# A four-layer diffusion backbone: attention probabilities scaled on GpSimd by a scalar per partition, and the sink logit taken as the first value of the fused row minimum

## The chip, the cores and the metric

The kernel runs on one core of one Trainium2 chip. The profile names the core's engines PE (TensorE matmuls), PEld (TensorE weight loads), DVE (VectorE), ACT (ScalarE), POOL (GpSimd) and SP (the queue that issues the DMAs). The metric is the device time of one launch in microseconds. Three runs of the kernel before took 2281.0, 2281.58 and 2281.96 us; the median is 2281.58 us.

## The reference, cut to what matters

Two token streams, 256 latent tokens and 256 context tokens of width 1024, go through four layers. Layer i mixes tokens by its kind (differential attention, neighbourhood attention, windowed grouped-query attention with a sink, differential attention again) and then runs a SwiGLU FFN; each half is normalised before and after. The change touches the softmax of the second and the third layer.

```
# layer 1, neighbourhood attention (16 heads of 64)
s_nb = q . k(neighbours) + relative-position bias;  s_cx = q . k(context)
p = softmax(concat[s_nb, s_cx]);  out = p . v
# layer 2, windowed attention (16 heads, 4 key heads) with a sink logit per head
s_band = where(valid, s_band, -inf)
snk = broadcast_to(sink_f, (B, KV, G, QB, 1))
p = softmax(concat([s_band, s_cx, snk], axis=-1))
out = p[..., :nband] @ v_band + p[..., nband:nband + C] @ v_cx      # the sink's column has no value row
# context rows attend to context keys alone, with the same sink in layer 2
```

## The kernel before, in words

The text calls the layers 0 to 3 (kinds A, B, C, A), the context stream c and the latent stream l. Tile names end in the same letters: `bkc` and `bkl` are PSUM banks, `x_c` and `x_l` the residual streams, `h` the normalised input in two halves. Each matrix product is made of three matmuls (`mm3`, lines 508 to 510): high part times high part, high times low, low times high. So every weight tile of 128x1024 is loaded by SP, split by ACT into a rounded part `wh` and by DVE into the rest `wl` (line 522).

A layer runs over units, one weight tile each: value, query and key projections, then the output projection (`o`), then 22 gate, 22 up and 22 down units of the FFN. In layers 1 and 2 each query and key pair of units is followed by `att_bc` for two heads. A head of the latent stream has two query tiles of 128 rows with 512 keys each; a head of the context stream has one tile in which two query blocks of 128 rows stand side by side with 256 keys each. One tile goes this way: scores on PE (887, 888); for the latent stream one fused DVE operation that adds the bias or mask, writes the sum and its negated row minimum (995), for the context stream a row maximum (895); in layer 2 a small DVE operation that takes the sink into that column (1001); exponential and row sum on ACT; in layer 2 the sink's exponential and an add (1018); reciprocal (1020); the scaling of the probabilities; four PE transposes (907); a split into two parts by ACT and DVE (915); the product with the values (1037, 1038) and the sum of its halves (1043). Before the change the scaling stood on POOL for the context stream (1023); for the latent stream the table `SPLIT` put it on DVE (1026) for both query tiles of layer 1 and for tile 0 of layer 2, and on ACT for tile 1 of layer 2.

After the output projection and after the FFN each stream passes a norm: ACT squares the output and DVE multiplies it by the gate (798), POOL makes the reciprocal root (690, 692), DVE adds to the residual (804), ACT squares again, POOL makes the second root, DVE scales (725), PE transposes (738), and ACT and DVE split the result into `h` (752). PE can only go on with that stream's next products after that; until then it works on the other stream.

The order of all instructions on every engine is made by a list scheduler in the program (`Plan`): the code records operations with an engine, a planned duration, a priority and the buffers that they touch; `run` schedules them four times with priorities mixed from the earlier passes, and the pass with the least planned end is emitted. Each engine executes its own list strictly in order. So a change of one planned duration moves instructions in all layers, on all engines.

Of the kernel before, what the change touches and what calls it, by code (L numbers as in the profile page):

```python
# [14 lines left out]
ALU = mybir.AluOpType  # L15
AX = mybir.AxisListType

P = 128
# [39 lines left out]
ALONE = 2  # L58
QK_BOTH = False
LATE = 5  # L60
SPLIT = {"B": [0, 1], "C": [0]}
BOOST = {"A": -4.0, "B": 8.0, "C": 16.0, "N": 20.0, "F": -8.0, "X": 28.0}
ADA_BANK = "bkc"
# [262 lines left out]
def t_dve(n, fast=False, extra=0.0):  # L326
    return 0.07 + (0.00052 if fast else 0.00104) * n + extra
# [3 lines left out]
def trunk(ctx: ExitStack, tc: tile.TileContext, a: dict, out: bass.AP, layers=tuple(range(DEPTH)), info=None):  # L331
    nc = tc.nc
# [43 lines left out]
    def fixed(shape, dt=F32, name="k"):  # L376
        return Buf("fixed", ap=const.tile(list(shape), dt, name=name, tag=name))
# [12 lines left out]
    def op(eng, dur, fn, reads=(), writes=(), p=None, also=()):  # L390
        r = [x if isinstance(x, tuple) else (x, None) for x in reads]
        w = [x if isinstance(x, tuple) else (x, None) for x in writes]
        return plan.op(eng, dur, fn, prio() if p is None else p, r, w, also)
# [18 lines left out]
    def dve(fn, dur, reads, writes, p=None):  # L412
        return op("dve", dur, fn, reads, writes, p)
# [4 lines left out]
    def load_fixed(shape, src, name):  # L418
        b = fixed(shape, name=name)
        dma(lambda: b.ap, lambda: src, 4 * int(np.prod(shape)), [], [b])  # L420
        return b
# [29 lines left out]
    late = {}  # L451

    def late_consts():

        late["cosT"] = load_fixed((P, T), a["cosT"], "cosT")
        late["sinT"] = load_fixed((P, T), a["sinT"], "sinT")
        late["sink"] = load_fixed((P, 16), a["c_sink"].to_broadcast([P, 16]), "sink")
        sub = late["subln"] = load_fixed((P, 2), a["sublnT"], "subln")
        lamv = Buf("f2")
        v4 = lambda: lamv.ap[:].rearrange("p (j f d) -> p j f d", j=2, f=4)  # L460
# [461 lines left out]
    def part(x, i, nk):  # L922
        return x.ap[:, i * nk:(i + 1) * nk]
# [50 lines left out]
    def att_bc(S, s, j, L):  # L974
        kind = MIXERS[L]
# [5 lines left out]
        nk = T * len(kp[0])  # L981
        nkt = nk // P
        sinks = kind == "C"
        vals = values(s)
        qs, o = S.qs, S.o
        for m in range(2):
            pt = pt_tiles(s, nkt)
            head = 2 * j + m
            for qts in blocks(s):
# [2 lines left out]
                e, l, nm, r = Buf("f2", cap=("e" + s, CAP_E[s])), Buf("col"), Buf("col"), Buf("col")  # L992
                sb = scores(s, qs, m, qts, kp[m], e)
                if plus:
                    dve(lambda e=e, sb=sb, plus=plus, nm=nm: nc.vector.tensor_tensor_reduce(
                        e.ap, sb.ap, plus.ap, -1.0, 3e38, ALU.add, ALU.min, nm.ap[:, 0:1]), t_dve(512), [sb, plus], [e, nm])
                else:
                    neg_max(sb, nm, nq)
                if sinks:
                    sink = late["sink"]  # L1000
                    dve(lambda nm=nm, head=head, nq=nq: nc.vector.scalar_tensor_tensor(
                        nm.ap[:, 0:nq], sink.ap[:, head:head + 1].to_broadcast([P, nq]), -1.0, nm.ap[:, 0:nq], ALU.mult, ALU.min),
                        0.08, [sink], [nm])
# [16 lines left out]
                dve(lambda r=r, l=l, nq=nq: nc.vector.reciprocal(r.ap[:, 0:nq], l.ap[:, 0:nq]), 0.1, [l], [r])  # L1020
                for i in range(nq):
                    if s == "c":
                        op("pool", 0.7, lambda e=e, r=r, i=i: nc.gpsimd.tensor_tensor(
                            part(e, i, nk), part(e, i, nk), r.ap[:, i:i + 1].to_broadcast([P, nk]), ALU.mult), [r], [(e, i)])
                    elif qts[0] in SPLIT[kind]:
                        dve(lambda e=e, r=r: nc.vector.tensor_scalar(e.ap, e.ap, r.ap[:, 0:1], None, ALU.mult),
                            t_dve(nk, True, 0.06), [r], [e])
                    else:
                        act(lambda e=e: e.ap, lambda e=e: e.ap, AF.Copy, t_act(nk, False, 1), [r], [e],
                            scale=lambda r=r: r.ap[:, 0:1])  # L1030
# [324 lines left out]
    for L in layers:  # L1355
        kind = MIXERS[L]
# [151 lines left out]
```

## Time and profile before

| What | Value |
|---|---|
| median of 3 runs | 2281.58 us (2281.0 to 2281.96) |
| the profiled execution | 2279.39 us |
| its span, first to last instruction | 2277.3 us |
| mean granted TensorE clock | 0.992 |
| busy: PE, PEld, DVE, ACT, POOL | 97%, 85%, 72%, 47%, 10% |
| on the chain that ended last: PE, DVE, ACT, POOL | 83%, 9%, 4%, 1% |

The profiled execution is 2.1 us longer than its span and 2.2 us below the median. The busy shares are means over stages that differ much: in the FFN stages PE is busy without a break, in the attention of layer 2 DVE is nearly so.

### The profile page before, as it was taken

What the parts mean: (1) busy time and instruction counts of PE and PEld (TensorE: products, weight loads), DVE (VectorE), ACT (ScalarE), POOL (GpSimd) and SP (SyncE); (2) the same over time, 40 slices, a digit from 0 to 9 for tenths busy, and PEclk for the clock granted to TensorE, in tenths of its full rate; (3) what the DMA queues carried; (4) which work ended last, traced back from release to release, by engine and by line L of the source; (5) the groups of instructions that cost most, each with busy time, mean ns of one, the idle gap of its engine ahead of it and who ended that gap; (6) DMA issues with size and microseconds to landing.
All of it is one profiled execution on the core that took longest, in us unless ns stands there. A gap on an engine that the chain in (4) does not pass through costs nothing.

```text
span 2277.3 us, 35872 instructions
## 1 busy us (share of the span) xinstructions
PE 2212.1 (97%) x13236; PEld 1929.4 (85%) x13236; DVE 1642.2 (72%) x3145; ACT 1062.0 (47%) x2245; POOL 221.6 (10%) x300
## 2 busy tenths in 40 slices
PE   7999999999999999999999999999999998998998
PEld 5889888888878998888878898888887887997997
DVE  4988698887354888878773489988778335896454
ACT  4478642223344776522233368862223324685443
POOL 0111110000010221200000133010000001320000
PEclk9999999999999999999999999999999999999999
DMA  8643366664233343556542430256654242434654
GB/s 294 214 131 121 98 202 221 213 215 149 86 123 93 103 114 107 179 193 210 191 153 93 138 87 19 75 160 204 213 187 172 87 136 75 128 114 148 185 184 141
DMA packets 369279, 338.92 MB, mean 149 GB/s; under 512 B 33120, under 2 KB 282960, under 8 KB 369104
## 3 DMA queue, kind: packets, MB, share of 16 engines
q1 hardware_dynamic: 369104, 336.63, 46.6%
q8 instruction: 104, 1.70, 0.3%
q14 instruction: 71, 0.58, 0.1%
HBM read 321.77 MB, written 1.17 MB: 142 GB/s over the span
## 4 chain that ended last, share of the span: by engine, by line
PE 83%; DVE 9%; ACT 4%; issue 2%; POOL 1%; DMA 0%; SPq 0%; DVEq 0%; ACTq 0%; POOLq 0%
PE bkl L508 19%; PE bkl L509 19%; PE bkl L510 19%; PE bkc L508 6%; PE bkc L509 6%; PE bkc L510 6%; ACT f L408 2%; PE bkl L907 1%; DVE r L915 1%; ACT r L408 1%; DVE wl L522 1%; PE bkc L636 1%; DVE col L895 1%; PE bkl L738 1%; DVE r L856 1%
## 5 line engine op out<-in xcount | busy, mean ns | idle before, releaser
L408 ACT ACTIVATE wh<-wr 128x1024 fp32r<-128x1024 f32 x380 | 402.6, 1061 | 843.1 <-PE bkl L509 499.1
L522 DVE TENSOR_TENSOR wl<-wr,wh 128x1024 fp32r<-128x1024 f32 x380 | 472.6, 1245 | 350.7 <-ACT wh L408 349.5
L508 PE MATMUL bkl<-h,wh 128*128 128x256 f32 (+1 forms) x1872 | 637.0, 340 | 0.0
L509 PE MATMUL bkl<-h,wh 128*128 128x256 f32 (+1 forms) x1872 | 632.2, 338 | 0.0
L510 PE MATMUL bkl<-h,wl 128*128 128x256 f32 (+1 forms) x1872 | 632.2, 338 | 0.0
L629 DVE SCALAR_TENSOR_TENSOR f<-f,cs,f 128x512 f32<-128x512 f32 x556 | 386.4, 745 | 6.0 <-DMA f<-in_ada_w 5.3
L508 PEld LDWEIGHTS bkl<-h,wh 128*128 128x128 f32 x1872 | 355.5, 190 | 41.5 <-issue 3.7
L510 PEld LDWEIGHTS bkl<-h,wl 128*128 128x128 f32 x1872 | 355.3, 190 | 37.5
L509 PEld LDWEIGHTS bkl<-h,wh 128*128 128x128 f32 x1872 | 355.5, 190 | 36.9
L508 PE MATMUL bkl<-wh,h 128*128 128x512 f32 (+1 forms) x560 | 219.1, 391 | 0.0
L509 PE MATMUL bkl<-wl,h 128*128 128x512 f32 (+1 forms) x560 | 216.7, 387 | 0.0
L510 PE MATMUL bkl<-wh,h 128*128 128x512 f32 (+1 forms) x560 | 216.6, 387 | 0.0
L508 PE MATMUL bkc<-wh,h 128*128 128x512 f32 (+1 forms) x472 | 186.6, 395 | 0.2 <-ACT j L408 0.2
L510 PE MATMUL bkc<-wh,h 128*128 128x512 f32 (+1 forms) x472 | 184.1, 390 | 1.8 <-DVE h L702 1.0
L509 PE MATMUL bkc<-wl,h 128*128 128x512 f32 (+1 forms) x472 | 183.9, 390 | 1.7 <-DVE wl L522 1.7
L690 POOL TENSOR_SCALAR col<-col 128x1 f32<-128x1 f32 x58 | 37.2, 642 | 1477.2 <-ACT j L408 1432.4
L509 PE MATMUL bkc<-h,wh 128*128 128x256 f32 x496 | 142.6, 287 | 6.6 <-DVE h L752 6.4
L508 PE MATMUL bkc<-h,wh 128*128 128x256 f32 x496 | 144.0, 290 | 0.2
L510 PE MATMUL bkc<-h,wl 128*128 128x256 f32 x496 | 141.7, 286 | 0.0
L508 PEld LDWEIGHTS bkl<-wh,h 128*128 128x128 f32 x560 | 105.4, 188 | 22.0 <-ACT h L408 0.8
L510 PEld LDWEIGHTS bkl<-wh,h 128*128 128x128 f32 x560 | 105.3, 188 | 21.4
L509 PEld LDWEIGHTS bkl<-wl,h 128*128 128x128 f32 x560 | 105.4, 188 | 19.8
(213 smaller groups left out, 3400.8 us busy)
## 6 DMA issues: line engine op xcount, KB each, us to landing
wr<-in_ffn_w SPq DMA_DIRECT2D x264, 512.0 KB, 3.7
f<-in_ada_w SPq DMA_DIRECT2D x384, 256.0 KB, 4.3
wr<-in_a_wqkv SPq DMA_DIRECT2D x48, 512.0 KB, 3.7
f<-gd SPq DMA_DIRECT2D x54, 256.0 KB, 4.8
r<-r SPq DMA_DIRECT2D x96, 128.0 KB, 2.3
wr<-in_b_wqkv SPq DMA_DIRECT2D x24, 512.0 KB, 3.6
wr<-in_a_wo SPq DMA_DIRECT2D x16, 512.0 KB, 3.5
wr<-in_c_wqkv SPq DMA_DIRECT2D x12, 512.0 KB, 3.7
```

Of the source, the lines that this page charges most:

```text
L408: nc.scalar.activation(o(), i(), func, **k)
L508: nc.tensor.matmul(o, lh, rh, start=first, stop=False)
L509: nc.tensor.matmul(o, lh, rl, start=False, stop=False)
L510: nc.tensor.matmul(o, ll, rh, start=False, stop=last)
L522: dve(lambda: nc.vector.tensor_tensor(l.ap, raw.ap, f32(h.ap[:]), ALU.subtract), t_dve(1024), [raw, h], [l], p)
L629: dve(lambda b=b, raw=raw, c=c: nc.vector.scalar_tensor_tensor(b.ap, raw.ap, c(), b.ap, ALU.mult, ALU.add), t_dve(512, extra=0.06), [raw, ...
L636: nc.tensor.matmul(acc.ap[32 * j:32 * j + 32, u * 256:(u + 1) * 256], lhs, tiles[j // 2].ap[:, (j % 2) * 256:(j % 2 + 1) * 256], start=fir ...
L690: op("pool", 0.25, lambda: nc.gpsimd.tensor_scalar(r.ap[:, 1:2], ss.ap[:, 0:1], ss.ap[:, 1:2], D * EPS, ALU.add, ALU.add), [ss], [r])
L738: nc.tensor.transpose(tp.ap[:, c0:c0 + P], xn[t, k // 4].ap[:, (k % 4) * P:(k % 4 + 1) * P], ident.ap)
L856: dve(lambda r0=r0, r1=r1, m=m: nc.vector.scalar_tensor_tensor(qs.ap[r1, m, :], src()[r0], QSCALE, f32(qs.ap[r0, m, :]), ALU.mult, ALU.sub ...
L895: dve(lambda: nc.vector.tensor_reduce(nm.ap[:, 0:n], b.ap[:].rearrange("p (i k) -> p i k", i=n), AX.X, ALU.max, negate=True), t_dve(512), ...
L907: nc.tensor.transpose(tp.ap[:, to * P:(to + 1) * P], e.ap[:, c * P:(c + 1) * P], ident.ap)
```

## The change

The diff has three edits.

1. A tile `negsink` holds the negated sink, made once by DVE. For latent rows of layer 2 the fused operation takes the head's column of it as the first value of its running minimum, in place of the constant 3e38, and the small operation of line 1001 goes for them (32 of 48; the 16 of the context stream stay).
2. The context stream's scaling on POOL (64 operations of 128x256 in layers 1 and 2 together) becomes a tensor_scalar with a column as its scalar, in place of a tensor_tensor with the column broadcast. Its planned duration goes from 0.7 to 0.5.
3. A table `ON_POOL` puts the scaling of latent query tile 0 in layer 2 (16 operations of 128x512) on POOL, planned at 0.85; these were on DVE.

```diff
+ON_POOL = {"B": [], "C": [0]}
...
+        negs = late["negsink"] = fixed((P, 16), name="negsink")
+        dve(lambda: nc.vector.tensor_scalar(negs.ap, late["sink"].ap, -1.0, None, ALU.mult), 0.1, [late["sink"]], [negs])
...
-                    dve(lambda e=e, sb=sb, plus=plus, nm=nm: nc.vector.tensor_tensor_reduce(
-                        e.ap, sb.ap, plus.ap, -1.0, 3e38, ALU.add, ALU.min, nm.ap[:, 0:1]), t_dve(512), [sb, plus], [e, nm])
+                    first = (lambda head=head: late["negsink"].ap[:, head:head + 1]) if sinks else lambda: 3e38
+                    dve(lambda e=e, sb=sb, plus=plus, nm=nm, first=first: nc.vector.tensor_tensor_reduce(
+                        e.ap, sb.ap, plus.ap, -1.0, first(), ALU.add, ALU.min, nm.ap[:, 0:1]), t_dve(512),
+                        [sb, plus] + ([late["negsink"]] if sinks else []), [e, nm])
...
-                if sinks:
-                    sink = late["sink"]
+                sink = late["sink"]
+                if sinks and not plus:
...
-                        op("pool", 0.7, lambda e=e, r=r, i=i: nc.gpsimd.tensor_tensor(
-                            part(e, i, nk), part(e, i, nk), r.ap[:, i:i + 1].to_broadcast([P, nk]), ALU.mult), [r], [(e, i)])
+                        op("pool", 0.5, lambda e=e, r=r, i=i: nc.gpsimd.tensor_scalar(
+                            part(e, i, nk), part(e, i, nk), r.ap[:, i:i + 1], None, ALU.mult), [r], [(e, i)])
+                    elif qts[0] in ON_POOL[kind]:
+                        op("pool", 0.85, lambda e=e, r=r: nc.gpsimd.tensor_scalar(e.ap, e.ap, r.ap[:, 0:1], None, ALU.mult), [r], [e])
```

The scheduler makes a new order from this. Three places are shown; the line numbers of the new kernel are a few higher (798, 804, 725 and 738 become 801, 807, 728 and 741).

On DVE at the end of the attention of layer 1, the context stream's norm before the FFN: the residual adds (804) and the scalings (725) of `x_c`. Before:

```order
L798 TENSOR_TENSOR f_10166<-bkc,f_10011 128x512
L804 SCALAR_TENSOR_TENSOR x_c<-f_10037,col,x_c 128x512
L804 SCALAR_TENSOR_TENSOR x_c<-f_10166,col,x_c 128x512
L798 TENSOR_TENSOR f_10192<-bkc,f_10011 128x512
L804 SCALAR_TENSOR_TENSOR x_c<-f_10054,col,x_c 128x512
L804 SCALAR_TENSOR_TENSOR x_c<-f_10192,col,x_c 128x512
L725 SCALAR_TENSOR_TENSOR f_10189<-x_c,col,f_10023 128x512
L725 SCALAR_TENSOR_TENSOR f_10204<-x_c,col,f_10035 128x512
L522 TENSOR_TENSOR wl<-wr,wh 128x1024 x2
```

And now, from the first residual add on (1000 is the fused minimum, 1034 the scaling of a latent tile, 918 and 1051 the split and the sum of halves of a latent head):

```order
L807 SCALAR_TENSOR_TENSOR x_c<-f_9918,col,x_c 128x512
L807 SCALAR_TENSOR_TENSOR x_c<-f_10051,col,x_c 128x512
L807 SCALAR_TENSOR_TENSOR x_c<-f_9920,col,x_c 128x512
L807 SCALAR_TENSOR_TENSOR x_c<-f_10066,col,x_c 128x512
L1026 RECIPROCAL col<-col 128x1
L1051 TENSOR_TENSOR ool<-bkl,f_10118 64x256
L1000 ISA f_10069,col<-bkl,f_122 128x512
L1000 ISA col 128x1
L1034 TENSOR_SCALAR f_10060<-f_10060,col 128x512
L728 SCALAR_TENSOR_TENSOR f_10110<-x_c,col,f_9905 128x512
L918 TENSOR_TENSOR r_10079<-bkl,r_10078 128x2x128
L728 SCALAR_TENSOR_TENSOR f_10120<-x_c,col,f_9905 128x512
```

Before, the last latent heads were done when the norm of the context stream ran, and 42 latent products of the output projection stood on PE beside it. Now the norm runs among the operations of the last latent heads.

On PE at the end of the output projection of layer 2, the transposes of the two norms (738, now 741; `bkc` and `bkl` tell the streams). Before:

```order
L738 MATMUL bkc<-ident,f_16155 128x128
L738 MATMUL bkc<-ident,f_16170 128x128
L508 MATMUL bkl<-wh,h_78 128x512
L509 MATMUL bkl<-wl,h_78 128x512
L510 MATMUL bkl<-wh,h_78 128x512
L508 MATMUL bkl<-wh,h_79 128x512
L509 MATMUL bkl<-wl,h_79 128x512
L510 MATMUL bkl<-wh,h_79 128x512
L738 MATMUL bkc<-ident,f_16167 128x128
L738 MATMUL bkc<-ident,f_16181 128x128
```

And now:

```order
L741 MATMUL bkc<-ident,f_16124 128x128
L741 MATMUL bkc<-ident,f_16200 128x128
L741 MATMUL bkl<-ident,f_16266 128x128
L741 MATMUL bkl<-ident,f_16273 128x128
L741 MATMUL bkl<-ident,f_16266 128x128
```

Before, 48 latent products stood ahead of the context stream's first transposes, and 60 products of the FFN's first context unit between its last ones and those of the latent stream. Now 30 latent products stand ahead, and the transposes of the two streams follow each other.

On POOL in the attention of layer 2, where the context stream's scalings (1023, now 1029), the rotary products (844 and 845, now 847 and 848) and the new scalings of latent tiles (1032) share one queue. Before, in the middle of the stage:

```order
L1023 TENSOR_TENSOR f_14359<-f_14359,col 128x256 x2
L844 TENSOR_TENSOR f_14487<-f_14487,sinT 128x256
L1023 TENSOR_TENSOR f_14390<-f_14390,col 128x256 x2
L845 TENSOR_TENSOR f_14476<-f_14476,f_14487 128x256
L1023 TENSOR_TENSOR f_14420<-f_14420,col 128x256 x2
L1023 TENSOR_TENSOR f_14479<-f_14479,col 128x256 x2
```

And now, at about the same place:

```order
L1032 TENSOR_SCALAR f_14274<-f_14274,col 128x512
L847 TENSOR_TENSOR f_14416<-f_14416,sinT 128x256
L1029 TENSOR_SCALAR f_14321<-f_14321,col 128x256 x2
L848 TENSOR_TENSOR f_14441<-f_14441,f_14416 128x256
L1032 TENSOR_SCALAR f_14303<-f_14303,col 128x512
L1029 TENSOR_SCALAR f_14342<-f_14342,col 128x256 x2
```

The latent scalings are new in the queue: each stands in turn with context scalings and rotary pairs, and one rotary pair still has a context tile's scaling between its two operations.

## Rows read from the trace of the kernel before

**Rows 1.** The page, its first part: the span; then busy time, share of the span and instructions of PE, PEld, DVE, ACT and POOL.

```profile
span 2277.3 us, 35872 instructions
PE 2212.1 (97%) x13236; PEld 1929.4 (85%) x13236; DVE 1642.2 (72%) x3145; ACT 1062.0 (47%) x2245; POOL 221.6 (10%) x300
```

**Rows 2.** Busy time by stage. Columns: window, its length, then PE, PEld, DVE, ACT and POOL busy (instructions), granted clock, DMA share, GB/s. The windows are the passage from layer 0 to 1; the attention of layer 1; its passage to the FFN; the attention of layer 2; its passage to the FFN; the passage from layer 2 to 3.

```profile
640.00:700.00 60.00, 56.73 (x279) 45.59 (x278) 35.76 (x62) 28.00 (x60) 10.66 (x16) 0.94 0.36 109
740.00:880.00 140.00, 138.45 (x1140) 136.09 (x1140) 124.23 (x302) 106.50 (x283) 35.53 (x53) 1.00 0.39 104
880.00:945.00 65.00, 62.59 (x353) 54.60 (x352) 49.82 (x100) 36.80 (x89) 15.06 (x20) 0.97 0.52 158
1360.00:1480.00 120.00, 111.15 (x811) 103.58 (x810) 113.67 (x382) 101.80 (x297) 23.99 (x35) 0.99 0.15 48
1480.00:1525.00 45.00, 42.67 (x272) 37.94 (x271) 38.60 (x74) 29.67 (x73) 11.01 (x16) 1.00 0.54 170
1868.00:1900.00 32.00, 25.76 (x113) 21.28 (x112) 24.76 (x39) 18.04 (x46) 10.11 (x16) 0.89 0.27 88
```

**Rows 3.** The operations that the change touches, and their neighbours on POOL. The first three rows are groups by line and shape over the whole run: busy us, mean ns | idle before. The others are single lines: count, then minimum, median and maximum in ns, first and last start in us.

```profile
L1026 DVE TENSOR_SCALAR f<-f,col 128x512 f32<-128x512 f32 x48 | 25.9, 541 | 0.8
L1001 DVE SCALAR_TENSOR_TENSOR col<-sink,col 128x1 f32<-128x1 f32 x32 | 4.3, 150 | 0.0
L995 DVE CUSTOM_DVE_ANT_0 f<-bkl,f 128x512 f32<-128x512 f32 x64 | 43.4, 681 | 4.4 <-POOL f L1068 1.7 <-PE bkl L888 1.3 <-issue 1.2
L1023 POOL TENSOR_TENSOR f<-f,col x64: 607/613/1700, 736.4 to 1409.2; 128x256 f32<-128x256 f32 x64
L690 POOL TENSOR_SCALAR col<-col x58: 299/302/2476, 10.3 to 2271.0; 128x1 f32<-128x1 f32 x58
L844 POOL TENSOR_TENSOR f<-f,sinT x42: 723/739/1802, 98.5 to 2037.9; 128x256 f32<-128x256 f32 x42
L845 POOL TENSOR_TENSOR f<-f,f x42: 723/874/1932, 99.9 to 2039.1; 128x256 f32<-128x256 f32 x42
```

**Rows 4.** Who PE waited for in the attention of layer 2 (1360 to 1480 us): total us, times, longest us.

```profile
PE bkl L907 <- DVE f L1026: 2.2, 1, 2.2
PE bkc L509 <- DVE wl L522: 1.7, 1, 1.7
PE bkl L887 <- DVE col L995: 1.7, 1, 1.7
PE bkc L907 <- POOL f L1023: 1.7, 2, 1.2
```

**Rows 5.** PE in order of time at the end of layer 2's output projection: start us, length, line and tiles, count [idle before, and who ended it]. The first row is the first of 48 latent products right behind the last context product, 1506.20 is the last latent product; L738 are the transposes of the two norms.

```profile
1491.47 0.39 PE L508 MATMUL bkl<-wh,h 128*128 128x512 f32 x1
...
1502.36 1.03 PE L738 MATMUL bkc<-ident,f 128*128 128x128 f32 x8
...
1506.20 0.39 PE L510 MATMUL bkl<-wh,h 128*128 128x512 f32 x1
...
1511.07 0.39 PE L509 MATMUL bkc<-h,wh 128*128 128x256 f32 x1 [1.74 <-DVE h L752]
...
1516.71 0.27 PE L738 MATMUL bkl<-ident,f 128*128 128x128 f32 x1
1517.44 0.98 PE L738 MATMUL bkl<-ident,f 128*128 128x128 f32 x7 [0.45 <-DVE f L725]
```

**Rows 6.** The same view at the end of layer 1's output projection. The first row is the last context product.

```profile
917.57 0.39 PE L510 MATMUL bkc<-wh,h 128*128 128x512 f32 x1
...
927.32 1.04 PE L738 MATMUL bkc<-ident,f 128*128 128x128 f32 x8
...
934.71 0.39 PE L509 MATMUL bkc<-h,wh 128*128 128x256 f32 x1 [0.86 <-DVE h L752]
...
936.81 0.58 PE L509 MATMUL bkc<-h,wh 128*128 128x256 f32 x1 [1.49 <-DVE h L752]
```

**Rows 7.** The same view at the other passages: from layer 0 to 1 (first two rows), from layer 2 to 3 (next two), and in layer 3, where only the latent stream is left, from its last output product to its transposes (last two).

```profile
673.36 0.29 PE L594 MATMUL bkc<-ident,c 128*32 128x128 f32 x1 [2.49 <-DVE c L603]
...
675.08 0.80 PE L510 MATMUL bkc<-wh,h 128*128 128x512 f32 x1 [0.78 <-DVE h L752]
...
1884.57 0.33 PE L738 MATMUL bkc<-ident,f 128*128 128x128 f32 x1 [4.04 <-DVE f L725]
1887.10 2.61 PE L738 MATMUL bkc<-ident,f 128*128 128x128 f32 x11 [2.20 <-DVE f L725]
...
2071.42 0.39 PE L510 MATMUL bkl<-wh,r 128*128 128x512 f32 x1
2078.84 0.45 PE L738 MATMUL bkl<-ident,f 128*128 128x128 f32 x1 [7.03 <-DVE f L725]
```

**Rows 8.** DVE operations of the norms and of a latent head's end, by line and shape over the whole run: busy us, mean ns | idle before.

```profile
L804 DVE SCALAR_TENSOR_TENSOR x_c<-f,col,x_c 128x512 f32<-128x512 f32 x24 | 16.8, 747 | 1.8 <-POOL col L692 1.8
L725 DVE SCALAR_TENSOR_TENSOR f<-x_c,col,f 128x512 f32<-128x512 f32 x24 | 17.0, 746 | 5.0 <-POOL col L692 5.0
L752 DVE SCALAR_TENSOR_TENSOR h<-bkc,mod,h 128x256 fp32r<-128x256 f32 x48 | 20.8, 475 | 1.6 <-ACT h L408 1.5
L915 DVE TENSOR_TENSOR r<-bkl,r 128x256 fp32r<-128x256 f32 x192 | 73.6, 415 | 6.6 <-ACT r L408 5.7
L1043 DVE TENSOR_TENSOR ool<-bkl,f 64x256 f32<-64x256 f32 x32 | 13.2, 413 | 3.4 <-ACT f L408 2.9
```

## The prediction

> **What bounds the kernel now.** I read the page's first part, then the busy time by stage, then PE in order of time where a stage shows PE idle. PE is busy 97% of the span [rows 1], and the FFN stages are solid, so a change can only win or lose where PE stands still or runs at its lower clock. Those places are few [rows 2]. The attention of layer 1 leaves PE 1.6 of 140 us idle. The attention of layer 2 leaves 8.9 of 120 us, while DVE is busy 113.7 us (95%) and ACT 101.8 (85%): this stage is DVE's. The passages between stages make up most of the rest: 3.3 us idle from layer 0 to 1, 2.4 at the end of layer 1's attention, 2.3 at that of layer 2, 6.2 from layer 2 to 3; in layer 3 one piece alone has 7.0 us [rows 7].
>
> At a passage PE waits for a norm. In layer 3 nothing covers it, and PE stands from the last output product to the first transposes, 2071.42 to 2078.84: 7.4 us for a bare norm of one stream [rows 7]. With two streams sharing DVE, ACT and POOL it is longer: from the last context product, just ahead of 1491.47, to 1502.36, at most 11 us, in layer 2, and from the last latent product at 1506.20 to 1517.44, 11.2 us [rows 5]. What stands on PE between a stream's last product and its transposes is its cover. The 48 latent products take 10.9 us (0.227 each), and there PE doesn't wait at all; 44 products of 256 columns take 5.6 us from 1511.07 to 1516.71, 0.13 each [rows 5].
>
> Idle time also costs clock: the granted clock is 0.94 over 60 us where PE stood 2.49 and 0.78 us, 0.97 over 65 us behind 0.86 and 1.49 us, 0.89 over 32 us behind 4.04 and 2.20 us, but 1.00 behind 1.74 and 0.45 us [rows 2, 5 to 7]. [...]
>
> **The change, part by part.** *Layer 2's attention.* DVE loses 16 scalings at 0.541 us, 8.7 us, and 32 sink minima at 0.150 us, 4.8 us [rows 3]: 13.5 of 113.7 us. The fused minimum reads its first value from a column in place of a constant; it took 0.681 us [rows 3], and I leave that. From below nothing less is to be expected; from above take the step between the two DVE forms of 512 columns with and without a column of which I have rows, 0.746 against 0.681 [rows 3, 8]: 0.07 us, 2 us over 32. PE waited here once 2.2 us for a DVE scaling, and 1.7 us each for a weight split and a row minimum [rows 4], all in DVE's queue. PE's idle 8.9 us and the 1.2 us that clock 0.99 costs are all that can come back. Two things limit it. ACT's 101.8 us don't shrink: in 106.5 us they would be 96%, so ACT is late next. And in the new order 84 output products, not 60, stand behind the last value product, so 5.5 us of PE work no longer fills the attention; 13.5 less 5.5 leaves 8 us. I take -5 us, from -10 to +4.
>
> The 16 scalings on POOL have no row of their own. Nearest from below is a tensor_scalar of one column, 0.302 us; from above two context tiles of 256, 2 x 0.613 us; with the fixed 0.30 us counted once, 0.93 us [rows 3]. I take 0.8 us, near the upper row since that one also moves a whole tile: 13 us more on POOL, which is busy 24 of 120 us [rows 2]. The head waits 0.3 us longer than the DVE scaling took, plus what POOL has in hand: behind the waiting scaling in its queue stand rotary pairs (0.74 and 0.87 us) and context scalings, and for these wait the next scores and context transposes. [...]
>
> *Context scalings.* 64 on POOL now take 0.613 us; the new form lies between one column's 0.302 and a rotary product's 0.739 us [rows 3]. At 0.5 us, midway from the first to today's, a tile of two saves 0.2 us. In layer 1 PE has 1.6 us idle to give; in layer 2 PE waited 1.7 us for them [rows 4], counted above. I take -0.5 us, from -1 to +0.5. `negsink` is one operation of 16 columns, once: nothing.
>
> *What the new order does to the passages.* No edit touches them, but the scheduler has moved their cover. I count products in the new order and set them against the norm's 7.4 to 11 us.
>
> From layer 0 to 1 the context stream's cover grows from 30 to 36 wide products and the latent one's from 12 to 24: 1.4 and 2.7 us against 3.3 us idle [rows 7]. Idle falls to 0 or 1 us, and part of the 3.6 us of clock comes back: -5 us, from -1 to -6.9.
>
> End of layer 1. Before, the context norm had 42 latent products beside it, 9.7 us from 917.57 to 927.32, and PE's two waits were for `h` [rows 6]. Now it has 8 score products, 16 head transposes, 24 value products and its own first 8 transposes until its second transposes: 32 x 0.13 and 24 x 0.13 [rows 5], 7.2 us. DVE, from the first residual add to the last scaling of that norm, has 4 adds, 4 scalings (725) and 2 parts of `h` of the norm itself, and of the latent heads 9 splits of 256 columns, 2 sums, 2 scalings and 1 fused minimum: 2.99 + 2.98 + 0.95 + 3.74 + 0.83 + 1.08 + 0.68 = 13.3 us [rows 3, 8]. PE would idle 6.1 us. Behind it 60 latent products cover the rest of the context norm, so the two waits for `h` (2.4 us [rows 6]) go; the latent norm then has 72 narrow products, 9.2 us, against 7.4 to 11, about 1 us short. 6.1 - 2.4 + 1 = +5 us, from 0 (DVE has started early) to +9 (clock lost as well).
>
> End of layer 2. The context norm has 30 products, 6.8 us, in place of 48. The latent norm has 16 transposes, 2 us, in place of 60 products and 4 transposes; 7.4 to 11 us less 2 leaves 5.4 to 9 us idle where there were 2.2 [rows 5]. That is 3.2 to 7 us more; I take 4, and 2 us for the clock, since the passages with over 2.3 us idle lost 2 to 3.6 us and this one none. +6 us, from +3 to +10.
>
> From layer 2 to 3 the latent transposes stand right behind the first 8 of the context stream, without the 12 wide products (2.7 us) between. PE already waits 6.2 us there [rows 7], which serves both norms. +2 us, from 0 to +4. Where the products and transposes stand at the entry to layer 2's attention the order is the same.
>
> **Sum.** -5 - 0.5 - 5 + 5 + 6 + 2 = +2.5 us. The profiled execution took 2279.4 us (span 2277.3 and 2.1 around it): 2281.9 us. The median of the runs lies 2.2 us above it: 2284.1 us.
>
> **The rivals.** *A, DVE's relief decides (2273 us).* If the norms at both ends run near their bare 7.4 us, the end of layer 1 costs 1, that of layer 2 4 and the passage to layer 3 1 us, and the attention of layer 2 gives back 9: -9 - 0.5 - 5 + 1 + 4 + 1 = -8.5 us. For it: DVE at 95% there is the clearest bound in the trace [rows 2]. Against it: ACT at 85%, and no norm with two streams was bare [rows 5].
>
> *B, the lost cover decides (2290.6 us).* The ends of layers 1 and 2 cost 8 and 9 us, the passage to layer 3 2.5, the rest as forecast: -5 - 0.5 - 5 + 8 + 9 + 2.5 = +9 us. It wins as soon as the two ends cost over 13 us together, when the gains of 10.5 are outrun by a margin that shows. For it: the norm chain took 11 us each time it had company, and idle time brings the lower clock. Against it: DVE may be ahead of PE when the norm begins.
>
> *C, POOL and DVE hold each other up (2290 us).* The same rotary operation takes from 0.723 to 1.932 us, and a context scaling from 0.607 to 1.700 [rows 3], so something holds POOL for up to 1.2 us. If the new scalings hold DVE as they are held, 16 x 0.8 = 13 us return what DVE was relieved of, and layer 2's attention gives +1 in place of -5. Against it: the medians (0.613 and 0.739) sit at the minima, so most are not held. [...]
>
> **Chances.** The forecast 0.42, A 0.22, B 0.27, C 0.09. The measurement can tell 0.2%, 4.6 us, from no change. Faster by more: most of A and a little of the forecast, 0.21. Slower by more: B, nearly all of C and the forecast's upper edge, 0.39. Within: 0.40. The range, 2275 to 2292 us, holds the forecast, B and C with some margin and leaves out about half of A and the worst of B.
>
> **What would show it.** In the profile after: DVE busy 100 us or so and PE idle under 5 us over layer 2's attention; the POOL scalings near 0.8 us; the fused minimum still 0.68 us; PE idle 5 to 9 us in one or two pieces between the last head of layer 1 and its output products, waiting for DVE 725 (now 728); 5 to 9 us at the end of layer 2 before the latent transposes, with a clock below 1.00 behind it; no idle piece over 1 us from layer 0 to 1. The prediction is wrong if layer 2's attention keeps its idle time, or if the ends of layers 1 and 2 wait no longer than before.

## The result, and the profile after

The changed kernel took 2295.95 us (median of 6 runs, 2294.39 to 2298.59), the kernel before 2280.38 us beside it (6 runs, 2278.52 to 2281.96). The ratio is 1.0068, 95% interval 1.0058 to 1.0078: slower by 0.7%, beyond the upper end of the predicted range, 2292.

The page of the kernel after, its first part, answers to [rows 1].

```profile
span 2292.6 us, 35870 instructions
PE 2213.9 (97%) x13236; PEld 1929.0 (84%) x13236; DVE 1631.4 (71%) x3098; ACT 1063.5 (46%) x2245; POOL 269.2 (12%) x316
```

PE does the same 13236 matmuls; 15.3 us of span are added. DVE is relieved by 10.8 us, POOL has 47.6 us more. The six stages of [rows 2], in the kernel after (the same columns; the windows follow the work, so some are longer):

```profile
640.00:700.00 60.00, 56.61 (x280) 45.60 (x279) 35.43 (x62) 27.64 (x60) 8.88 (x16) 0.94 0.36 112
735.00:875.00 140.00, 136.74 (x1106) 132.59 (x1106) 120.19 (x289) 101.26 (x268) 48.81 (x56) 1.00 0.42 109
875.00:945.00 70.00, 63.91 (x364) 56.29 (x363) 51.86 (x109) 40.51 (x99) 12.44 (x20) 0.95 0.42 126
1362.00:1482.00 120.00, 112.71 (x835) 104.75 (x834) 110.74 (x344) 106.55 (x307) 61.00 (x53) 1.00 0.16 51
1482.00:1527.00 45.00, 39.27 (x232) 34.86 (x231) 35.03 (x64) 27.21 (x65) 9.12 (x16) 0.92 0.49 157
1875.00:1912.00 37.00, 27.20 (x116) 22.01 (x115) 25.82 (x41) 18.99 (x48) 9.80 (x16) 0.82 0.32 99
```

The third, fifth and sixth rows are the passages: 6.1, 5.7 and 9.8 us of PE idle, and the clock at 0.95, 0.92 and 0.82. In the fourth, layer 2's attention, DVE has 3 us less work and PE still idles 7.3 us.

Since the windows don't hold quite the same work, I also set the two traces against each other at equal PE work: each matmul counts with one duration for its shape (0.227, 0.120 and 0.109 us for 512, 256 and 128 columns; less for the narrow ones of layer 0), and the times are compared at which both kernels have done the same sum. After against before, stage by stage: to the end of layer 0 -4.9; passage from layer 0 to 1 +0.1; layer 1's attention +3.3; its end +4.3; layer 2's attention -0.9; its end +4.9; passage from layer 2 to 3 +4.9; layer 3 +3.5. With the FFN stages (+0.1) that is +15.3 us, but for rounding. "At equal work" means this below. Each figure rests on one trace of each kernel: traces of kernels below that share an order and, in a stage, all instructions differ there by some 1 us, once by 3 (by the end of layer 0).

PE in order of time, kernel after: the waits of over 0.7 us at the passages from layer 0 to 1, at the ends of layers 1 and 2, and from layer 2 to 3. They answer to [rows 5 to 7].

```profile
666.90 0.27 PE L597 MATMUL bkc<-ident,c 128*32 128x128 f32 x1 [0.83 <-DVE c L606]
670.64 0.80 PE L513 MATMUL bkc<-wh,h 128*128 128x512 f32 x1 [2.56 <-DVE h L755]
...
916.36 1.11 PE L910 MATMUL bkl<-ident,f 128*128 128x128 f32 x4 [4.18 <-DVE f L1034]
...
924.67 1.07 PE L741 MATMUL bkc<-ident,f 128*128 128x128 f32 x8 [1.38 <-DVE f L728]
...
1508.12 1.86 PE L741 MATMUL bkc<-ident,f 128*128 128x128 f32 x15 [0.87 <-DVE f L728]
1513.86 0.48 PE L741 MATMUL bkl<-ident,f 128*128 128x128 f32 x1 [3.89 <-DVE f L728]
1515.31 1.75 PE L741 MATMUL bkl<-ident,f 128*128 128x128 f32 x7 [0.97 <-DVE f L728]
...
1890.32 0.33 PE L741 MATMUL bkc<-ident,f 128*128 128x128 f32 x1 [2.86 <-DVE f L728]
1892.58 1.75 PE L741 MATMUL bkc<-ident,f 128*128 128x128 f32 x7 [1.93 <-DVE f L728]
1898.62 0.47 PE L741 MATMUL bkl<-ident,f 128*128 128x128 f32 x1 [4.29 <-DVE f L728]
1899.81 1.76 PE L741 MATMUL bkl<-ident,f 128*128 128x128 f32 x7 [0.72 <-DVE f L728]
```

The wait of 4.18 us is for the scaling of a latent head (L1034), which stands on DVE among the context norm's operations; for that norm's own scaling (L728) PE waits another 1.38 us. From 1890 on each stream's norm is waited for by itself, 4.8 and 5.0 us.

The changed operations, kernel after, by line and shape (busy us, mean ns | idle before), answer to [rows 3]; the last row is the fused minimum that starts from the sink's column.

```profile
L1029 POOL TENSOR_SCALAR f<-f,col 128x256 f32<-128x256 f32 x64 | 63.2, 1001 | 71.7 <-DVE col L1026 43.7 <-PE bkl L512 11.1 <-DVE col L1021 4.9
L1032 POOL TENSOR_SCALAR f<-f,col 128x512 f32<-128x512 f32 x16 | 28.2, 1763 | 33.6 <-DVE col L1026 15.2 <-ACT wh L409 10.5 <-ACT f L409 4.4
L1000 DVE CUSTOM_DVE_ANT_0 f<-bkl,f,negsink 128x512 f32<-128x512 f32 x32 | 23.6, 741 | 2.4 <-PE bkl L891 2.2
```

As single instructions, the context scaling takes 915, 923 and 1972 ns (minimum, median, maximum), the latent one 1562, 1566 and 2953. So the form with a column is the slower one on POOL: 923 ns against 613 for the broadcast product [rows 3]. In layer 2's attention (1290 to 1480 us), PE waited for them and for DVE as follows (total us, times, longest us).

```profile
PE bkc L910 <- POOL f L1029: 4.9, 10, 1.2
PE bkl L910 <- POOL f L1032: 3.1, 3, 1.8
PE bkl L511 <- DVE f L846: 0.6, 1, 0.6
PE bkl L1046 <- DVE r L918: 0.6, 1, 0.6
PE bkc L890 <- DVE r L859: 0.5, 1, 0.5
```

So in this stage PE's waits for DVE fell from 6.7 to 1.6 us, and its waits for POOL rose from 1.7 [rows 4] to 8.0.

### The profile page after: what moved, and what is told of

Its sections match the earlier page's. It is cut to its first block, busy times and chain, and to the rows that moved or that the text cites. A ratio compares the mean times of both kernels' runs of the same rounds, so it can differ in the third digit from the quotient of the medians.

```text
span 2292.6 us, 35870 instructions
## 1 busy us (share of the span) xinstructions
PE 2213.9 (97%) x13236; PEld 1929.0 (84%) x13236; DVE 1631.4 (71%) x3098; ACT 1063.5 (46%) x2245; POOL 269.2 (12%) x316
## 4 chain that ended last, share of the span: by engine, by line
PE 83%; DVE 7%; ACT 4%; POOL 2%; issue 2%; DMA 1%; SPq 0%; DVEq 0%; POOLq 0%; ACTq 0%
PE bkl L511 19%; PE bkl L513 19%; PE bkl L512 19%; PE bkc L511 6%; PE bkc L513 6%; PE bkc L512 6%; ACT f L409 2%; ACT r L409 1%; PE bkl L910 1%; PE bkc L639 1%; DVE wl L525 1%; DVE r L918 1%; POOL f L1029 1%; PE bkl L890 1%; PE bkl L891 1%
```

## The experiments

Two theories stood at the start. ORDER: the scheduler's new order costs the time, whatever instructions stand in it. OPS: the slow scalings on POOL cost it. Twelve kernels were run; ratios are against the kernel before on the same chip.

### The new instructions in the old order, and the reverse

`new_ops_old_order`: before, its planned durations untouched, so that PE, ACT and SP keep their lists; only what is issued differs.

```diff
-                        op("pool", 0.7, lambda e=e, r=r, i=i: nc.gpsimd.tensor_tensor(
-                            part(e, i, nk), part(e, i, nk), r.ap[:, i:i + 1].to_broadcast([P, nk]), ALU.mult), [r], [(e, i)])
+                        op("pool", 0.7, lambda e=e, r=r, i=i: nc.gpsimd.tensor_scalar(
+                            part(e, i, nk), part(e, i, nk), r.ap[:, i:i + 1], None, ALU.mult), [r], [(e, i)])
...
-                        dve(lambda e=e, r=r: nc.vector.tensor_scalar(e.ap, e.ap, r.ap[:, 0:1], None, ALU.mult),
+                        eng = nc.gpsimd if kind == "C" else nc.vector
+                        dve(lambda e=e, r=r, eng=eng: eng.tensor_scalar(e.ap, e.ap, r.ap[:, 0:1], None, ALU.mult),
```

The sink's edit is in it too, as below. `old_ops_new_order`: after, with the old instructions of the three edits issued at the new places.

```diff
+                    def fused(e=e, sb=sb, plus=plus, nm=nm, head=head):
+                        nc.vector.tensor_tensor_reduce(
+                            e.ap, sb.ap, plus.ap, -1.0, 3e38, ALU.add, ALU.min, nm.ap[:, 0:1])
+                        if sinks:
+                            nc.vector.scalar_tensor_tensor(
+                                nm.ap[:, 0:1], late["sink"].ap[:, head:head + 1], -1.0, nm.ap[:, 0:1], ALU.mult, ALU.min)
...
-                        op("pool", 0.85, lambda e=e, r=r: nc.gpsimd.tensor_scalar(e.ap, e.ap, r.ap[:, 0:1], None, ALU.mult), [r], [e])
+                        op("pool", 0.85, lambda e=e, r=r: nc.vector.tensor_scalar(e.ap, e.ap, r.ap[:, 0:1], None, ALU.mult), [r], [e])
```

> All three edits' instructions, but emitted at the places of the order of before: PE, ACT and SP lists are those of before, word for word. Theory ORDER (the scheduler's new order cost the time, at the passages between stages): 2277 to 2285 us, within 0.2% of before; PE's waits at the ends of layers 1 and 2 stay at 2.4 and 2.2 us. Theory OPS (the GpSimd tensor_scalar, 0.92 us for 256 and 1.57 us for 512 columns in the trace after, cost it): 2290 us or more, with the loss inside the attention of layers 1 and 2.

> The instructions of before (broadcast tensor_tensor on GpSimd, both sinks' small operations, tile 0 scaled on DVE), emitted at the places of the order of after. ORDER: 2289 to 2296 us, with the waits of after at the ends of layers 1 and 2 and from layer 2 to 3. OPS: 2278 to 2285 us.

Measured: the new instructions in the old order 2281.58 us, 1.0007 [0.9999, 1.0016]; the old instructions in the new order 2295.79 us, 1.0070 [1.0058, 1.0082]. The order carries the whole loss. Its waits at the passages, PE in order of time, are those of after to 0.03 us; three of them:

```profile
914.04 1.11 PE L910 MATMUL bkl<-ident,f 128*128 128x128 f32 x4 [4.18 <-DVE f L1039]
...
1513.88 0.48 PE L741 MATMUL bkl<-ident,f 128*128 128x128 f32 x1 [3.89 <-DVE f L728]
...
1899.13 0.47 PE L741 MATMUL bkl<-ident,f 128*128 128x128 f32 x1 [4.30 <-DVE f L728]
```

Yet the new instructions gained nothing in the old order either. Their window of layer 2's attention (columns of [rows 2]) and PE's waits for POOL there:

```profile
1290.00:1480.00 190.00, 178.87 (x1317) 166.94 (x1317) 163.11 (x452) 148.27 (x416) 82.10 (x84) 1.00 0.23 69
```

```profile
PE bkl L912 <- POOL f L1033: 3.7, 3, 1.4
PE bkc L912 <- POOL f L1029: 3.7, 4, 1.4
```

The same window of before:

```profile
1290.00:1480.00 190.00, 180.30 (x1323) 169.24 (x1322) 171.47 (x501) 148.30 (x417) 47.35 (x68) 0.99 0.23 70
```

DVE is busy 8.4 us less and PE no more: it waits 7.4 us for POOL instead, against 1.7 [rows 4]. In the new order they moved time from one stage to another: at equal work `old_ops_new_order` is 1.5 us behind before in layer 2's attention, where after is 0.9 ahead, but 1.8 us behind in layer 1's, where after is 3.3 behind.

### The sink's edit alone

`sink_old_order`: edit 1 alone, in the order of before. The small operation keeps its place in the plan and issues nothing for latent rows; `negsink` is made inside an operation that is there already.

```diff
-                    dve(lambda nm=nm, head=head, nq=nq: nc.vector.scalar_tensor_tensor(
+                    dve(lambda nm=nm, head=head, nq=nq, plus=plus: None if plus else nc.vector.scalar_tensor_tensor(
```

> Edit 1 alone at the places of the order of before: the fused minimum starts at the sink, 32 small DVE operations of 0.15 us are gone from layer 2. ORDER and OPS alike: 2275 to 2281 us, 0 to 5 us less than before, the fused minimum at 0.68 us. If the column as first value makes the fused operation dearer, the time rises instead.

2280.34 us, 1.0006 [0.9995, 1.0017]: no gain. In its trace the fused minimum takes 740 ns in place of 681 (741 in the kernel after), so of 4.8 us of small operations 32 x 0.06 = 1.9 us come back.

### The form of the scaling in the new order

`tt_new_order`: after, with every scaling on POOL issued as the broadcast product.

```diff
-    nc.gpsimd.tensor_scalar(e.ap, e.ap, r.ap[:, 0:1], None, ALU.mult)
+    nc.gpsimd.tensor_tensor(e.ap, e.ap, r.ap[:, 0:1].to_broadcast([P, nk]), ALU.mult)
```

> After with one thing changed: every GpSimd scaling is a tensor_tensor with the column broadcast (same order). Context tiles should take 0.61 us again and latent tiles 0.9 to 1.25 us. ORDER: 2288 to 2295 us, at most 5 us less than after. OPS: under 2286 us.

2291.45 us, 1.0050 [1.0038, 1.0062], 4.5 us less than after in the medians; the two intervals just overlap. The same groups as above:

```profile
L1029 POOL TENSOR_TENSOR f<-f,col 128x256 f32<-128x256 f32 x64 | 41.8, 678 | 80.6 <-DVE col L1026 44.7 <-PE bkl L512 11.1 <-DVE col L1021 5.4
L1032 POOL TENSOR_TENSOR f<-f,col 128x512 f32<-128x512 f32 x16 | 18.3, 1147 | 39.9 <-DVE col L1026 14.1 <-ACT wh L409 11.0 <-ACT f L409 5.1
```

PE's waits for POOL in layer 2's attention fall from 8.0 to 2.3 us, those for DVE rise from 1.6 to 3.5:

```profile
PE bkl L910 <- POOL f L1032: 1.6, 2, 1.0
PE bkc L910 <- POOL f L1029: 0.7, 2, 0.3
```

### What turned the order

`replan_05`: before, with nothing changed but one planned duration.

```diff
-                        op("pool", 0.7, lambda e=e, r=r, i=i: nc.gpsimd.tensor_tensor(
+                        op("pool", 0.5, lambda e=e, r=r, i=i: nc.gpsimd.tensor_tensor(
```

`after_true`: after, planned with durations near the measured ones.

```diff
-                        op("pool", 0.5, lambda e=e, r=r, i=i: nc.gpsimd.tensor_scalar(
+                        op("pool", 0.95, lambda e=e, r=r, i=i: nc.gpsimd.tensor_scalar(
...
-                        op("pool", 0.85, lambda e=e, r=r: nc.gpsimd.tensor_scalar(
+                        op("pool", 1.6, lambda e=e, r=r: nc.gpsimd.tensor_scalar(
```

> The kernel before with one number changed: the planned duration of the context scaling is 0.5 in place of 0.7. Every instruction is that of before; only the order differs, and the covers at the passages come out as in after (3.2 us at the end of layer 1, 1.7 us for the latent norm of layer 2, 1.0 us from layer 2 to 3). Theory NUMBER (the wrong planned duration alone turned the order): 2289 to 2296 us. Rival EDITS (the removed and moved operations turned it): within 0.3% of before.

> The kernel after with two numbers changed: the GpSimd scalings are planned at what they took in the trace after, 0.95 and 1.6, in place of 0.5 and 0.85. Same instructions as after. In its order the covers at all passages are those of before. NUMBER: 2277 to 2285 us. EDITS: 2290 us or more.

`replan_05`: 2294.45 us, 1.0063 [1.0046, 1.0080]. A number that no engine sees costs 0.63%, some 14 us. Its waits, PE in order of time:

```profile
915.39 0.66 PE L907 MATMUL bkl<-ident,f 128*128 128x128 f32 x4 [4.18 <-DVE f L1026]
...
1513.94 0.47 PE L738 MATMUL bkl<-ident,f 128*128 128x128 f32 x1 [4.22 <-DVE f L725]
...
1899.11 0.48 PE L738 MATMUL bkl<-ident,f 128*128 128x128 f32 x1 [4.29 <-DVE f L725]
```

`after_true`: 2272.71 us, 0.9972 [0.9962, 0.9982]: faster than both kernels. At each passage its order has the cover of before. At equal work it gains 2.9 us by the end of layer 0 and 5.3 in layer 2's attention. The first isn't shown to be the order's: three kernels below that share this order, with the same instructions in that layer, stand at 0.0 to -1.4 us there. In layer 2's attention it has, as window and as PE's only wait for POOL:

```profile
1290.00:1480.00 190.00, 184.86 (x1362) 172.74 (x1361) 170.29 (x471) 153.80 (x432) 86.73 (x84) 1.00 0.24 70
```

```profile
PE bkc L910 <- POOL f L1029: 1.8, 2, 1.0
```

PE does 4.6 us more work in the window than before, and the slow scalings (still 1.04 and 1.69 us in the mean) are waited for 1.8 us, not 8.0.

### Does cover alone set a passage?

`sink_replan`: edit 1 alone, with the order left to the scheduler (after, with edits 2 and 3 taken back). `before_norm`: before, with the planned durations of the norm's operations raised, which makes the scheduler put more work beside them. The second's edit, two of its seven lines:

```diff
-        op("pool", 0.25, lambda: nc.gpsimd.tensor_scalar(r.ap[:, 1:2], ss.ap[:, 0:1], ss.ap[:, 1:2], D * EPS, ALU.add, ALU.add),
+        op("pool", 0.5, lambda: nc.gpsimd.tensor_scalar(r.ap[:, 1:2], ss.ap[:, 0:1], ss.ap[:, 1:2], D * EPS, ALU.add, ALU.add),
...
-                        t_dve(512, extra=0.06), [(xb[s], (t, h)), r, G[h]], [b])
+                        t_dve(512, extra=0.36), [(xb[s], (t, h)), r, G[h]], [b])
```

> Edit 1 alone, as the change writes it, and the scheduler free to reorder. Its covers: 6.9 and 7.2 us (before 9.5 and 8.1) at the end of layer 0, 10.9 and 10.5 (8.2 and 5.1) from layer 0 to 1, 6.8 and 7.2 (9.5 and 8.1) at the end of layer 1, 9.5 and 4.6 (10.9 and 7.6) at that of layer 2, 11.0 and 10.8 (5.6 and 4.2) from layer 2 to 3. By the cover rule: +3, -5, +3, +2, -8 and -2 for the attention of layer 2, 2268 to 2276 us. If covers don't set the time, within 0.2% of before.

> The kernel before, same instructions, with the planned durations of the norms' operations raised (GpSimd 0.25 and 0.4 to 0.5 and 0.8, each ACT square and each DVE operation of 512 columns by 0.3), so that the scheduler leaves more cover: 15.0 and 13.2 us from layer 0 to 1, 13.7 and 14.1 from layer 2 to 3, 13.6 and 6.1 at the end of layer 2, 9.5 and 8.9 at that of layer 1, but 5.4 and 4.6 at that of layer 0. By the cover rule: -6, -9, 0, 0 and +7: 2268 to 2276 us, with no wait over 1 us from layer 2 to 3 and no lower clock there. If covers don't set the time, within 0.2% of before.

Both missed, the first by 10 us, the second by 1. `sink_replan` 2285.9 us, 1.0029 [1.0017, 1.0041]; `before_norm` 2277.09 us, 0.9989 [0.9979, 0.9998]. The passages where cover grew gained as expected: at equal work -6.0 and -8.5 us from layer 0 to 1 and 2 to 3 in the first, -5.1 and -7.5 in the second. But at the ends of attentions new waits stood. In `sink_replan`, at the ends of layers 0 and 2:

```profile
283.04 0.50 PE L510 MATMUL bkl<-wh,h 128*128 128x512 f32 x1 [3.27 <-ACT h L408]
...
315.08 3.20 PE L740 MATMUL bkl<-ident,f 128*128 128x128 f32 x15 [2.67 <-DVE f L727]
...
1519.72 0.58 PE L510 MATMUL bkc<-h,wh 128*128 128x256 f32 x1 [4.84 <-ACT h L408]
```

The first and the last are for `h` on its way to the next products, the second is for the latent norm's transposes. The two ends came with +7.0 and +7.2 us. In `before_norm`, at the same ends:

```profile
293.08 0.48 PE L738 MATMUL bkc<-ident,f 128*128 128x128 f32 x1 [3.81 <-DVE f L725]
...
1512.49 0.58 PE L509 MATMUL bkc<-h,wh 128*128 128x256 f32 x1 [3.78 <-DVE h L752]
```

There it cost +1.5 us at the end of layer 0, where +7 was expected, and +3.8 at that of layer 2, where nothing was. So cover ahead of the transposes didn't set the time alone: PE also waited for `h` behind them. How much cover that split needs was not tried.

### What of the fast version gains

Three kernels in the order of `after_true`: `old_ops_true_order` issues the old instructions of all three edits, `tile0_dve_true_order` puts only latent tile 0 back on DVE, `after_true_tt` issues the POOL scalings as broadcast products. `after_tt_plan` is the last one planned with its own durations, which makes another order. Against `after_true`, first `tile0_dve_true_order`, then `after_tt_plan` (`after_true_tt` has 0.95 and 1.6 in it):

```diff
-                        op("pool", 1.6, lambda e=e, r=r: nc.gpsimd.tensor_scalar(e.ap, e.ap, r.ap[:, 0:1], None, ALU.mult), [r], [e])
+                        op("pool", 1.6, lambda e=e, r=r: nc.vector.tensor_scalar(e.ap, e.ap, r.ap[:, 0:1], None, ALU.mult), [r], [e])
```

```diff
-                        op("pool", 0.95, lambda e=e, r=r, i=i: nc.gpsimd.tensor_scalar(
-                            part(e, i, nk), part(e, i, nk), r.ap[:, i:i + 1], None, ALU.mult), [r], [(e, i)])
+                        op("pool", 0.7, lambda e=e, r=r, i=i: nc.gpsimd.tensor_tensor(
+                            part(e, i, nk), part(e, i, nk), r.ap[:, i:i + 1].to_broadcast([P, nk]), ALU.mult), [r], [(e, i)])
...
-                        op("pool", 1.6, lambda e=e, r=r: nc.gpsimd.tensor_scalar(e.ap, e.ap, r.ap[:, 0:1], None, ALU.mult), [r], [e])
+                        op("pool", 1.2, lambda e=e, r=r: nc.gpsimd.tensor_tensor(
+                            e.ap, e.ap, r.ap[:, 0:1].to_broadcast([P, nk]), ALU.mult), [r], [e])
```

> The order of after_true on every engine, with the instructions of before in the places of the changed ones (sink minimum apart on DVE, context scaling as the broadcast product on GpSimd, latent tile 0 scaled on DVE). after_true gained 7.7 us, 5.3 of them in layer 2's attention. Theory INSTRUCTIONS (the three edits are what gains, once the order leaves the passages alone): nearly all of the gain goes, 2277 to 2282 us, PE idle again about 9 of the 120 us in layer 2's attention. Rival ORDER (the plan with 0.95 and 1.6 happens to be a better order, whatever stands in it): 2271 to 2275 us, PE idle 4 to 5 us there. I lean to INSTRUCTIONS, 0.6.

> The order of after_true, with the 16 scalings of latent tile 0 issued on DVE in place of GpSimd; sink edit and context scalings stay. Theory TILE 0 (taking 8.7 us of scaling off DVE is what gains in layer 2's attention): half or more of the gain goes, 2276 to 2281 us. Rival SINK (the 32 small minima that go are enough, and the scaling costs on DVE what it cost on GpSimd): 2271 to 2275 us. In the order of before neither edit gained, so it may also be that either alone frees DVE enough. I lean to SINK, 0.5, since a scaling of 1.6 us on GpSimd holds its head longer than one of 0.54 us on DVE.

> The order of after_true, every GpSimd scaling as a broadcast product instead of the form with a column: 0.25 us less for 256 columns and 0.4 us for 512. Theory PRICE (the scalings on GpSimd stand on the path in this order too, as they did in the order of the changed kernel, where the same exchange gave 4.5 us): 2 to 5 us less than after_true, 2267.5 to 2271 us. Rival COVERED (an order planned with the long durations hides them): within 1.5 us of after_true, 2271 to 2274.5 us. I lean to PRICE, 0.55.

> The same instructions as after_true_tt, but planned with their own durations (0.7 and 1.2 in place of 0.95 and 1.6), so that the scheduler makes its own order: it comes out with the covers of sink_replan (context and latent norm at the end of layer 0's attention 6.9 and 7.2 us, at layer 1's 6.8 and 7.2, at layer 2's 9.5 and 4.6, layer 2 to 3 11.0 and 10.8), not with those of before. Theory TRUTH (durations near the measured ones give an order that wins): 2268 to 2274 us. Rival LOTTERY (any number that the scheduler is given draws one of a few orders, and what it costs is set by the passages of that order, not by how true the number is): some 10 us behind after_true_tt, 2279 to 2286 us, with PE idle pieces of 3 us or more at the ends of the attentions of layers 0 and 2, as sink_replan had. I lean to LOTTERY, 0.75.

| Kernel | us | ratio, 95% interval |
|---|---|---|
| old_ops_true_order | 2282.64 | 1.0007 [0.9999, 1.0016] |
| tile0_dve_true_order | 2276.57 | 0.9982 [0.9974, 0.9991] |
| after_true_tt | 2279.24 | 0.9996 [0.9987, 1.0004] |
| after_tt_plan | 2283.97 | 1.0014 [1.0004, 1.0023] |

INSTRUCTIONS holds for the gain: without the edits the fast order is no faster than before, and PE idles 9.3 of the 120 us in layer 2's attention, as that theory had it (4.3 in `after_true`). Between TILE 0 and SINK it stays open: with tile 0 back on DVE the median lies in TILE 0's band, but 0.0018 of the 0.0028 is kept, and the two intervals overlap.

PRICE fell, and in the other direction: POOL's shorter operations made the kernel slower by 0.0024. DVE operations of layer 2's attention (1290 to 1480 us, by line and shape), in `after_true`:

```profile
L918 DVE TENSOR_TENSOR r<-bkl,r 128x256 fp32r<-128x256 f32 x64 | 24.3, 415 | 2.6 <-ACT r L409 2.4
...
L1024 DVE TENSOR_TENSOR col<-col 128x1 f32<-128x1 f32 x32 | 5.6, 181 | 0.1
...
L1311 DVE TENSOR_TENSOR h<-ooc,h 128x256 fp32r<-128x256 f32 x8 | 3.7, 465 | 0.0
...
L1311 DVE TENSOR_TENSOR h<-ool,h 128x256 fp32r<-128x256 f32 x7 | 2.9, 410 | 0.0
```

and in `after_true_tt`:

```profile
L918 DVE TENSOR_TENSOR r<-bkl,r 128x256 fp32r<-128x256 f32 x54 | 20.8, 414 | 1.5 <-ACT r L409 1.3
...
L1024 DVE TENSOR_TENSOR col<-col 128x1 f32<-128x1 f32 x32 | 7.1, 228 | 0.1
...
L1312 DVE TENSOR_TENSOR h<-ool,h 128x256 fp32r<-128x256 f32 x6 | 4.1, 686 | 0.0
...
L1312 DVE TENSOR_TENSOR h<-ooc,h 128x256 fp32r<-128x256 f32 x8 | 3.3, 410 | 0.0
```

Beside the broadcast products eight of the fifteen groups of DVE's operations on SBUF tiles run longer (two of them: 181 to 228 ns, 410 to 686), the split that reads PSUM (`bkl`) doesn't (415 to 414); the one for `ooc` goes the other way (465 to 410). Over all DVE operations of the stage on SBUF tiles, counted alike, the exchange adds 6.0 us here, and 4.6 us in the order of after; over those that read PSUM it adds nothing in either. Here PE's waits for DVE rise from 2.2 to 5.6 us while those for POOL fall only from 1.8 to 0.6, and the kernel loses 4.9 us in the stage at equal work. In the order of after the waits for POOL fell by 5.7 us, which outweighed the 1.9 us more for DVE. That DVE is held by POOL's form is the reading that these rows suggest; no run measured it by itself.

LOTTERY holds, at a smaller price than expected (4.7 us behind `after_true_tt`, not 10): truer planned numbers for the broadcast form gave a worse order than the false ones, with the wait of `sink_replan` again:

```profile
1518.70 0.58 PE L511 MATMUL bkc<-h,wh 128*128 128x256 f32 x1 [4.84 <-ACT h L409]
```

So true numbers alone don't make an order fast. `after_true` drew one that keeps the covers of before, and in which PE waits little for the slow scalings. Why a planned duration turns the order of passages hundreds of microseconds away, inside the four passes of the scheduler, was not tried.

## Why the prediction was wrong

It forecast 2284.1 us from a sum of +2.5; the sum was +15.3. Its main idea, that the cover lost at the passages outweighs what the edits gain, held; four terms were off, and two stages were missing.

- **End of layer 1, +5, and of layer 2, +6: right.** They measured +4.3 and +4.9. At the end of layer 1 the prediction had PE wait 6.1 us for 728; it waited 4.18 us for a latent head's scaling in the same DVE queue and 1.38 us for 728. The waits for `h` went, as forecast. The 1 us that the latent norm was to be short did not come, and the clock, counted at nothing, was lower instead (0.95 over 70 us, 0.97 over 65 before), so part of the agreement there is luck. At the end of layer 2 the idle pieces grew from 2.2 to 5.7 us, 3.5 where 4 was taken.
- **From layer 2 to 3, +2 from 0 to +4: mis-sized, +4.9.** The step that the 6.2 us which PE already waits there [rows 7] serve both norms failed. Without the 12 products between them the two norms were waited for one after the other (2.86 + 1.93 and 4.29 + 0.72 us), and the clock fell to 0.82.
- **From layer 0 to 1, -5: failed, +0.1.** The step set cover against the norm alone. The idle piece ahead of the transposes shrank from 2.49 to 0.83 us, but that for `h` grew from 0.78 to 2.56 [rows 7], and the granted clock stayed at 0.94. The clock's share in this step, 3.6 us, is 0.06 x 60, one less the granted clock times the window, and the 2 us for the clock at the end of layer 2 were set by such losses; that rule was an estimate of mine which no run shows as it stands. In the trace of before, 512-column products follow each other every 0.427 us at a granted clock of 0.50 (677 to 679 us) and every 0.227 us at 1.00 (683 to 685), so 0.47 of the time is lost there, not 0.50.
- **Layer 2's attention, -5 from -10 to +4: mis-sized, -0.9.** The fused minimum costs 0.06 us more, close to the bound of 0.07 that I named and did not take. The step that failed most is POOL's price: 0.8 us taken, 0.93 as the upper bound, 1.566 us measured; the bound had two broadcast products as its dearest neighbour, and the form with a column is dearer (923 against 613 ns for 128x256). What PE no longer waited for DVE (6.7 to 1.6 us) it waited for POOL (1.7 to 8.0), and 7.3 us of the idle time stayed, one of the two signs that the prediction had named for being wrong. Rival C came near in size here, +1 us, but not by its mechanism: it had the scalings on POOL hold DVE, and DVE's busy time over the run fell by 10.8 of the 11.6 us that the edits take off it (8.7 + 4.8 - 1.9).
- **Context scalings, -0.5: wrong sign.** They were to take 0.5 us and take 0.923. Layer 1's attention lost 3.3 us at equal work. With the broadcast products `replan_05` lost 1.5 there, and in the very order of after `old_ops_new_order` lost 1.8 and `tt_new_order` 1.9, so about half is the order's and the rest the form's, as far as single traces can tell.
- **Not counted:** the end of layer 0 (-4.9) and layer 3 (+3.5). Both come with the order: `replan_05` has -4.3 and +3.8. I compared the orders only where the edits and the largest idle pieces stood.

Rival B, the lost cover, came nearest in kind, and at 2290.6 us in size; even it took the gain from layer 0 to 1 for granted. One line of the diff, the planned duration 0.7 that became 0.5, is enough for nearly all of the order's cost (1.0063 in `replan_05`, 1.0070 in `old_ops_new_order`). The prediction named it nowhere among its steps: it read the order's effects from place to place, and not what had moved them.

## What to carry to other kernels

Where a scheduler orders the program, a planned duration is itself an edit: run the old instructions in the new order and the new ones in the old order before judging the operations, and keep an order by its measured passages, not because its numbers are true. Before moving work to GpSimd, measure the very form there; the form with a column, which looks the simpler one, was slower here than the broadcast product (923 against 613 ns for 128x256). At a passage count the cover ahead of the transposes and that ahead of the first product that needs `h`, in every layer.

## What the runs showed of the hardware

On POOL a multiplication by a column took 923 ns for 128x256 and 1566 ns for 128x512 (medians in after, 2.5 ns per column between them), the broadcast product 613 ns for 128x256 (median in before). In the means the column form took 1001 and 1763 ns in after, the broadcast product 678 and 1147 ns in `tt_new_order`. On DVE the fused minimum took 60 ns more with a column as its first value (741 against 681 ns). The broadcast products on POOL went with longer DVE operations on SBUF tiles (6.0 and 4.6 us in sum, in two orders) and unchanged ones on PSUM (415 to 414 ns for the split of a latent head). In `after_true_tt`, against `after_true`, the operation of two columns went from 181 to 228 ns, the reciprocal of one column stayed at 152, and the operation for `ooc` went from 465 to 410. Why the shorter of POOL's two forms goes with the longer DVE operations, these runs leave open.
